# A fourth seven-product unit in gate and up, and low parts formed by adding transfers, in a float32 encoder block on Trainium2

## The chip, the cores and the metric

The kernel is one program on 1 core of one Trainium2 chip. The metric is the device time of one execution in microseconds. TensorE multiplies, VectorE, ScalarE and GpSimd work on data in SBUF (VectorE and ScalarE on PSUM too), SyncE issues the transfers of the weights; GpSimd issues most of the small ones. The engines run side by side, each through its own list of instructions in order, and wait for one another by semaphores.

## The reference, cut to what matters

One layer of an encoder on 256 tokens of width 2048, in float32: four mixers, cross attention, and a gated feed-forward network of width 5632.

```python
def swiglu(h, w_gate_up, w_down):
    gate, up = jnp.split(h @ w_gate_up, 2, axis=-1)
    return (jax.nn.silu(gate) * up) @ w_down

def reference(...):
    mem_n = rms_norm(mem, mem_norm_g)
    ...
    x = x + mix @ w_out[l]
    x = x + cross_attention(rms_norm(x, norm_g[l, 1]), mem_n, w_xq[l], w_xkv[l], w_xo[l])
    x = x + swiglu(rms_norm(x, norm_g[l, 2]), w_gate_up[l], w_down[l])
    return rms_norm(x, final_norm_g)
```

The change lies in `h @ w_gate_up`: 256 x 2048 by 2048 x 11264.

## The kernel before, in words

**Products in three parts.** A float32 operand is split into a high part, rounded to the matmul's format (`wh` for a weight), and a low part, the difference (`wl`). A product is three matmuls: high by high, high by low, low by high (`part`). ScalarE casts the high part (`nc.scalar.copy`), VectorE subtracts for the low part; both are in `Stream.split`.

**The stream of weights.** All weights come through one stream (`Stream`), in the order in which TensorE uses them, as slabs of 128 x 2048 (1 MB). A slab lands in a tile `raw` (three buffers, and in gate and up a fourth for every fourth slab) by a transfer on SyncE's queue, and is split in parts. A plain slab has two parts of 1024 columns; each part takes a buffer for `wh` and one for `wl`. In gate and up there are five such pairs: three in pool `wp`, two in `wp2`. `look` makes parts ahead as long as a pair is free. A pair is free again when TensorE has used the part.

**Gate and up.** Eleven groups `j`, each 512 columns of gate and the same 512 of up, for two blocks of 128 tokens; a group runs over eight slabs `i`, each two blocks `k` of 128 rows of the weights by 1024 columns. Four banks of PSUM (`cs`) collect the sums of a group. A plain slab is 2 x 2 x 2 products of 128 x 128 by 128 x 512, 24 matmuls.

**Units of seven.** Some slabs are multiplied as a 2 x 2 block product with seven products for eight (`unit`, `take_forms`): 21 matmuls. Sums of blocks of the weights are formed by VectorE in place in `raw` (`make`: one step on 1024 columns, two on 512), and the slab is split in four parts, of 512, 1024, 1024 and 1024 columns. Sums of blocks of the activations are formed once, in group 0 (`left`, inside `gate_up`). Four more banks collect what the units of a group share; `combine` adds them up after the last unit. `sevens(j)` says which slabs are units: slab 5 in group 0, slabs 1, 3 and 5 in groups 1 to 10. Units are used in the product with `w_down` as well, which the change leaves alone.

**The end of a group.** `finish` adds `cs` and the units' sums on VectorE, applies SiLU on ScalarE, multiplies, turns the result with VectorE's transpose into a tile `u`, and stores it by GpSimd's queue to `hidden` in DRAM in eight transfers (`store_turned`). It belongs to the next group's slabs 0 and 1, and must be done before that group's first unit begins, which needs the banks.

**GpSimd's queue.** It carries the stores of `keys`, of `values`, of `hidden` and of `xrows` (the residual, turned, in gate and up), and the reads of those back into SBUF.

**What sets the order.** The kernel is written as one list of steps. Side work is written as generators that are polled between matmuls (`Background`). The framework then orders the instructions of each engine by its own estimate of times; `keep_place` adds a dependency on the instruction just ahead on the same engine, so that a step stays where it was written. The steps of the units are kept so; the parts of plain slabs in gate and up are not. The keys are the first product of the kernel: three `gemm_rows` over `w_xkv`, the first with two columns of 512, whose four banks are turned by four transposes in `store_turned`, kept in place.

Of the kernel before, what the change touches and what calls it, by code (L numbers as in the profile page):

```python
# [14 lines left out]
F32R = mybir.dt.float32r  # L15
# [3 lines left out]
ALU = mybir.AluOpType  # L19
# [3 lines left out]
P = 128  # L23
# [25 lines left out]
GU = 16 * (40 + 16 + 16 + 32 + 16)  # L49

def sevens(j):

    return (1, 3, 5) if j else (5,)


FORMED = 6
# [20 lines left out]
DOWN = GU // 16 + 16 * DFF // 1024  # L77
# [6 lines left out]
def seven(slab):  # L84

    j, i = divmod(slab - GU // 16, 8)
    return slab in UNITS if slab >= DOWN else j >= 0 and i in sevens(j)
# [19 lines left out]
PI_LO = float(np.nextafter(np.float32(math.pi), np.float32(0)))  # L107


class Stream:  # L110


# [32 lines left out]
                return pool  # L145
        return None

    def split(self, pool, at, r, edges):

        nc = self.nc  # L150
        wh, wl = (pool.tile([P, 1088], F32R, name=t, tag=t) for t in ("wh", "wl"))
        wh, wl = wh[:, at:at + 1024], wl[:, at:at + 1024]
        for a, b in zip(edges, edges[1:]):
            nc.scalar.copy(wh[:, a:b], r[:, a:b])  # L154
            nc.vector.tensor_tensor(out=wl[:, a:b], in0=r[:, a:b], in1=wh[:, a:b].bitcast(F32), op=ALU.subtract)  # L155
        self.bg.dve(edges[-1], len(edges) - 1)
        self.items.append((pool, wh, wl))

    def make(self):

        nc, (slab, part) = self.nc, self.todo
        n = 16 * slab + 8 * part
        if n >= NBLK - HELD:
            parts = [(self.places.pop(0)) for _ in range(2)]
            r = self.raw(slab)[:, part * 1024:part * 1024 + 1024]
            for a, (wh, wl) in zip((0, 512), parts):
                nc.scalar.copy(wh, r[:, a:a + 512])
                nc.vector.tensor_tensor(out=wl, in0=r[:, a:a + 512], in1=wh.bitcast(F32), op=ALU.subtract)
            self.bg.dve(1024, 2)
            self.items.append((None, parts))  # L170
            self.todo = (slab + part, 1 - part)
            return True
        pool = self.free(slab)
        if pool is None:
            return False
        raw = self.raw(slab)
        at = 48 if any(a <= n < b for a, b in ROWS) else 8
        r = raw[:, part % 2 * 1024:part % 2 * 1024 + 1024]
        if not seven(slab):
            mark = len(nc.cur_bb.bb.instructions)  # L180
            self.split(pool, at, r, [0, 256, 512, 1024] if n == 0 else [0, 512, 1024] if n == 8 else [0, 1024])
            if DOWN <= slab < DOWN + 2 * AHEAD:
                self.keep(mark)
            self.todo = (slab + part, 1 - part)
            return True
        mark = len(nc.cur_bb.bb.instructions)
        op = lambda out, a, b, what=ALU.subtract: nc.vector.tensor_tensor(out=out, in0=a, in1=b, op=what)  # L187
        self.split(pool, at, r, [0, 512] if part == 0 else [0, 1024])
        b11, b12, b22, b21 = (raw[:, a:a + 512] for a in range(0, 2048, 512))
        if part == 0:  # L190
            blk = raw.rearrange("p (b c) -> p b c", b=4)
            op(r.rearrange("p (b c) -> p b c", b=2), blk[:, 0:3:2, :], blk[:, 1:2, :].to_broadcast([P, 2, 512]))
            self.bg.dve(1024)
        elif part == 1:
            op(b22, b22, b11, ALU.add)
            op(b21, b21, b22)
            self.bg.dve(1024, 2)
        self.keep(mark)
        self.todo = (slab + part // 3, (part + 1) % 4)
        return True  # L200
# [87 lines left out]
class Block:  # L288
# [286 lines left out]
    def mixers(self):  # L575
        tc, nc, act = self.tc, self.nc, self.act
# [76 lines left out]
        with tc.tile_pool(name="mid", bufs=1) as mid:  # L653
            self.dgp = mid
            gl = Gla(self, mid)
            with tc.tile_pool(name="hyp", bufs=1) as hyp, tc.tile_pool(name="k2", bufs=8) as k2:
                hy = Hyena(self, hyp, k2)

                mem0 = hy.piece()[:, 0:R + 16]
                nc.sync.dma_start(mem0, self.t["mem0"])  # L660
                self.bg.add(prepare(mid))

                for cols in ([0, 512], [1024], [1536]):
                    first = dict(parts=[[k] for k in range(KT)], before=start_m) if len(cols) > 1 else {}
                    for c, ps in zip(cols, self.gemm_rows("w_xkv", cols, h, **first)):
                        for r in range(2):
                            self.store_turned(self.kd[c:c + 512, r * P:(r + 1) * P], hy.piece(), ps[r][:, :], True)
                    if first:
                        for k in range(0, KT, 4):
                            self.load_x(k, 4)  # L670
                for hd in range(4):
                    for r, p in enumerate(self.gemm_rows("w_xkv", [D + hd * 512], h, start_x if hd == 3 else rows.append)[0]):
                        for c in range(2):
                            v, o = self.tmp(), (2 * hd + r) * 512 + c * R
                            nc.scalar.activation(v, p[:, c * R:(c + 1) * R], AF.Copy, scale=self.rcm[:, r:r + 1])
                            nc.gpsimd.dma_start(self.vd[:, o:o + R], v)
                self.bg.drain()

                def ev_u(i, p):
                    hy.feed(i, self.merge(p))  # L680
                    if i == 4:
                        self.bg.add(hy.convs())

                self.gemm("w_in", [UH + i * P for i in range(12)], h, ev_u)
                for r, p in enumerate(self.gemm_rows("w_in", [512], h, lambda k: k or low_rank())[0]):
                    nc.scalar.copy(gl.v[r], p)
                self.gemm("w_in", [256, 384, 0, 128], h, lambda i, p: gl.feed(i, self.merge(p)))
                self.gemm("w_in", scols[0:NSC], h, ev_s, narrow=True)
                self.bg.drain()

            with tc.tile_pool(name="glp", bufs=1) as glp:
                gl.open(glp)
                fn = Fnet(self, glp, act[20:24])
                g_gla = self.bg.add(gl.mix(act[4:8]))
                fn.feed(self.gemm_rows("w_in", [UF], h)[0])
                g_fn = self.bg.add(fn.mix(act[0:4], gl))
                self.gemm("w_in", scols[NSC:], h, lambda i, p: ev_s(i + NSC, p))
                g_sc = self.bg.add(self.group_norm(self.res[1], 2, act[20:24]))

                def ev_gate(i, p):  # L700
                    nc.scalar.activation(gl.gate[i], p[:, 0:R], AF.Silu)

                self.gemm("w_in", [1024 + i * P for i in range(4)], h, ev_gate, narrow=True)
                gl.done = True
                self.out_proj(lambda n: [self.bg.drain(g) for g in ((g_gla,), (g_fn, g_sc), ())[n]])
# [245 lines left out]
    def gate_up(self, sw, gp, f):  # L951

        nc, st = self.nc, self.st
# [6 lines left out]

        def left():

            for i in (5, 1, 3):
                t = [self.tmp() for _ in range(2)]
                for x, k in zip(t, (2 * i, 2 * i + 1)):
                    nc.scalar.activation(x, self.resk(k), AF.Copy, scale=self.gvec(V_NG + 32, k))
                (a11, a21), (a12, a22) = ((x[:, 0:P], x[:, P:R]) for x in t)
                s = gp.tile([P, 512], F32, name="u", tag="u", bufs=2)
                s1, s2, s3, s4 = (s[:, a:a + P] for a in range(0, 512, P))
                self.stt(s1, a21, -1.0, a22, ALU.mult, ALU.subtract)  # L970
                self.stt(s2, s1, -1.0, a11, ALU.mult, ALU.subtract)
                self.tt(s3, a11, a21, ALU.subtract)
                self.tt(s4, a12, s2, ALU.subtract)
                yield
                h, l = sums[i] = [sw.tile([P, 512], F32R, name=f"s{x}{i}") for x in "hl"]
                self.split2(h, l, s)
                yield
# [44 lines left out]

        ready = [self.late, self.bg.add(norm())]
        forms = self.bg.add(left())
        turned = self.bg.add(self.turn())
        early = end = None
        for j in range(DFF // 512):
# [5 lines left out]
            for i in range(8):  # L1033
# [7 lines left out]
                if i in sevens(j):  # L1041
                    if i == sevens(j)[0]:
                        if j == 0:
                            self.bg.drain(forms)
                        ps = [banks[1 - j % 2]() for _ in range(4)]
# [6 lines left out]
                for k in (2 * i, 2 * i + 1):  # L1052
                    for c in range(2):
                        wh, wl = st.take("w_gate_up", k, cols[c], 4)
# [804 lines left out]
```

## Time and profile before

| | |
|---|---|
| median of 3 runs | 1458.29 us (1456.57 to 1458.53) |
| the profiled execution | 1457.18 us |
| its span | 1455.3 us |
| TensorE busy | 1440.2 us, 99% of the span |
| VectorE busy | 1192.2 us, 82% |
| ScalarE busy | 844.1 us, 58% |
| GpSimd busy | 172.2 us, 12% |
| granted TensorE clock, mean | 0.997 |

In the rows of the profile PE is TensorE's matmul, PEld its loading of weights, DVE VectorE, ACT ScalarE, POOL GpSimd, SP SyncE. A row of the timeline has its start in us from the start of the span, its duration, the engine, the line of the kernel, the operation, the tile written and those read, and in brackets the idle time ahead of it with what ended it. Durations of matmuls overlap: their pace is read from their starts. A row of a stretch has its length and the busy time of each engine in it, the granted clock, and the share and rate of the transfers. A row of transfers has the tile, the queue, the number, the size of one and the median us from issue to landing. Matmuls into `pg` and `pm` are those into two sets of four banks, between which the groups of gate and up alternate.

### The profile page before, as it was taken

How to read it: one execution, taken by the hardware profiler on the slowest of the kernel's cores; microseconds unless marked ns; L12 is line 12 of the kernel's file. 1: busy time of each engine (PE TensorE's matmuls, PEld its weight loads, DVE VectorE, ACT ScalarE, POOL GpSimd, SP SyncE). 2: the span in 40 equal slices, each digit the busy share in tenths (PEclk: the TensorE clock that was granted, in tenths of full speed). 3: DMA queues.
4: the chain of work that ended last, by engine and by line, in shares of the span. 5: the costliest groups of instructions: out<-in, count | busy, mean ns of one | idle time of the engine just before them, and what ended most of it. 6: DMA issues, size and time to landing. Idle time of an engine off the chain costs nothing.

```text
span 1455.3 us, 19732 instructions
## 1 busy us (share of the span) xinstructions
PE 1440.2 (99%) x7219; PEld 1217.8 (84%) x7219; DVE 1192.2 (82%) x1748; ACT 844.1 (58%) x1252; POOL 172.2 (12%) x294
## 2 busy tenths in 40 slices
PE   9999999999999999999999999999999999999997
PEld 7788888888899888888888888888888888788886
DVE  6577768777868867877778999999999997988875
ACT  6466665456646656665555565555555654655554
POOL 0220100000000001110003334112111112100000
PEclk9999999999999999999999999999999999999999
DMA  9885654444535555555556767656667656545554
GB/s 351 283 314 192 229 193 169 174 158 167 206 122 203 204 200 203 185 174 177 199 191 221 252 234 245 241 191 244 234 228 248 207 198 235 216 183 200 224 203 145
DMA packets 57394, 307.16 MB, mean 211 GB/s; under 512 B 9774, under 2 KB 11471, under 8 KB 25681
## 3 DMA queue, kind: packets, MB, share of 16 engines
q1 hardware_dynamic: 45920, 281.11, 54.2%
q0 software_dynamic: 10944, 24.14, 5.5%
q8 instruction: 56, 0.92, 0.2%
q10 hardware_dynamic: 432, 0.66, 0.1%
q14 instruction: 42, 0.34, 0.1%
HBM read 291.71 MB, written 14.16 MB: 210 GB/s over the span
## 4 chain that ended last, share of the span: by engine, by line
PE 96%; DVE 2%; ACT 1%; issue 0%; DMA 0%; SPq 0%; ACTq 0%; DVEq 0%
PE pg L439 19%; PE pg L490 13%; PE pg L491 13%; PE pg L492 13%; PE pg L440 10%; PE pm L490 7%; PE pm L492 7%; PE pm L491 7%; PE pm L1360 1%; DVE wl L155 1%; PE pg L436 1%; PE pg L437 1%; PE pm L890 1%; PE pm L863 1%; ACT wh L154 0%
## 5 line engine op out<-in xcount | busy, mean ns | idle before, releaser
L154 ACT CAST wh<-raw 128x1024 fp32r<-128x1024 f32 (+1 forms) x589 | 589.2, 1013 | 473.1 <-PE pg L492 147.3
L155 DVE TENSOR_TENSOR wl<-raw,wh 128x1024 fp32r<-128x1024 f32 (+1 forms) x589 | 681.8, 1176 | 183.7 <-ACT wh L154 178.0
L439 PE MATMUL pg<-act,wh 128*128 128x512 f32 x1104 | 387.5, 393 | 0.0
L440 PE MATMUL pg<-act,wl 128*128 128x256 f32 x1216 | 340.7, 280 | 0.0
L490 PE MATMUL pg<-wh,act 128*128 128x512 f32 (+1 forms) x689 | 269.6, 392 | 2.3 <-DVE k L520 2.0
L491 PE MATMUL pg<-wl,act 128*128 128x512 f32 (+1 forms) x689 | 268.8, 390 | 1.2 <-DVE wl L155 1.1
L492 PE MATMUL pg<-wh,act 128*128 128x512 f32 (+1 forms) x689 | 268.8, 390 | 0.0
L439 PEld LDWEIGHTS pg<-act,wh 128*128 128x128 f32 x1104 | 207.4, 188 | 45.0
L440 PEld LDWEIGHTS pg<-act,wl 128*128 128x128 f32 x1216 | 228.5, 188 | 0.8 <-DVE wl L155 0.5
L490 PEld LDWEIGHTS pg<-wh,act 128*128 128x128 f32 x689 | 129.7, 188 | 31.0 <-ACT dgh L410 2.4
L491 PEld LDWEIGHTS pg<-wl,act 128*128 128x128 f32 x689 | 129.6, 188 | 29.2 <-DVE wl L155 2.5
L492 PEld LDWEIGHTS pg<-wh,act 128*128 128x128 f32 x689 | 129.7, 188 | 27.3
L491 PE MATMUL pm<-wl,act 128*128 128x512 f32 x318 | 123.7, 389 | 0.0
L492 PE MATMUL pm<-wh,act 128*128 128x512 f32 x318 | 123.7, 389 | 0.0
L490 PE MATMUL pm<-wh,act 128*128 128x512 f32 x318 | 123.6, 389 | 0.0
L187 DVE TENSOR_TENSOR raw<-raw 128x1024 f32<-128x1024 f32 x129 | 111.8, 866 | 3.0
L525 POOL DMA_DIRECT2D hidden<-u x88 | 56.8, 653 | 164.6 <-DVE u L520 141.9
L492 PEld LDWEIGHTS pm<-wh,act 128*128 128x128 f32 x318 | 59.7, 188 | 12.5
L491 PEld LDWEIGHTS pm<-wl,act 128*128 128x128 f32 x318 | 59.7, 188 | 12.4
L490 PEld LDWEIGHTS pm<-wh,act 128*128 128x128 f32 x318 | 59.7, 188 | 12.4
L1072 POOL DMA_DIRECT2D xrows<-tmp x64 | 37.0, 585 | 183.5 <-DVE rc L321 126.6
L936 POOL DMA_DIRECT2D tmp<-hidden x44 | 24.5, 560 | 141.2 <-DVE f L317 73.0
(353 smaller groups left out, 1773.1 us busy)
## 6 DMA issues: line engine op xcount, KB each, us to landing
raw<-in_W SPq DMA_DIRECT2D x246, 1024.0 KB, 4.9
raw<-in_W SPq DMA_DIRECT2D x11, 512.0 KB, 7.5
hidden<-u POOLq DMA_DIRECT2D x88, 64.0 KB, 4.4
tmp<-hidden POOLq DMA_DIRECT2D x44, 128.0 KB, 4.2
res<-in_xT SPq DMA_DIRECT2D x8, 512.0 KB, 7.5
k<-in_mem SPq DMA_DIRECT2D x8, 256.0 KB, 6.5
k<-in_x SPq DMA_DIRECT2D x8, 256.0 KB, 7.7
keys<-k POOLq DMA_DIRECT2D x32, 64.0 KB, 5.3
```

The lines of the kernel that those rows point to most:

```text
L154: nc.scalar.copy(wh[:, a:b], r[:, a:b])
L155: nc.vector.tensor_tensor(out=wl[:, a:b], in0=r[:, a:b], in1=wh[:, a:b].bitcast(F32), op=ALU.subtract)
L187: op = lambda out, a, b, what=ALU.subtract: nc.vector.tensor_tensor(out=out, in0=a, in1=b, op=what)
L436: self.nc.tensor.matmul(p[:, 0:R], wh, slot[:, 0:R], start=start, stop=False)
L439: self.nc.tensor.matmul(p[:, :], wh, slot[:, :], start=start, stop=False)
L440: self.nc.tensor.matmul(p[:, 0:R], wl, slot[:, 0:R], start=False, stop=stop)
L490: self.nc.tensor.matmul(p, hi, wh, start=start, stop=False)
L491: self.nc.tensor.matmul(p, hi, wl, start=False, stop=False)
L492: self.nc.tensor.matmul(p, lo, wh, start=False, stop=stop)
L525: nc.gpsimd.dma_start(to[:, :, 32 * a:32 * a + 32], u[32 * a:32 * a + 32, :].rearrange("f (b t) -> f b t", t=32))
L936: self.nc.gpsimd.dma_start(m[k], self.ff[k * P:(k + 1) * P, :])
L1072: nc.gpsimd.dma_start(to[:, :, c:c + 32], u[32 * a:32 * a + 32, :].rearrange("t (b f) -> t b f", f=32))
```

## The change

Three edits.

In groups 1 to 10 of gate and up slab 4 becomes a unit; `left` forms the sums of activations for it.

In the same groups the second half of each plain slab (0, 2, 6 and 7; `added`) gets its low part without VectorE: ScalarE writes the negated and rounded weights into `wl`, and a transfer on GpSimd's queue adds the unrounded weights from `raw` to it, in SBUF. ScalarE's cast into `wh` comes after the negation. The first halves keep VectorE's subtraction.

In the keys, the four transposes of the first `gemm_rows` are no longer kept in their place.

```diff
 def sevens(j):
-    return (1, 3, 5) if j else (5,)
+    return (1, 3, 4, 5) if j else (5,)

+def added(slab):
+    j, i = divmod(slab - GU // 16, 8)
+    return j >= 1 and slab < DOWN and i not in sevens(j)

-    def split(self, pool, at, r, edges):
+    def split(self, pool, at, r, edges, added=False):
         nc = self.nc
         wh, wl = (pool.tile([P, 1088], F32R, name=t, tag=t) for t in ("wh", "wl"))
         wh, wl = wh[:, at:at + 1024], wl[:, at:at + 1024]
+        if added:
+            nc.scalar.mul(wl, r, -1.0)
+            nc.gpsimd.dma_start(wl, r.bitcast(F32R), accum_op=ALU.add)
+            nc.scalar.copy(wh, r)
+            self.items.append((pool, wh, wl))
+            return
         for a, b in zip(edges, edges[1:]):
...
-            self.split(pool, at, r, [0, 256, 512, 1024] if n == 0 else [0, 512, 1024] if n == 8 else [0, 1024])
+            self.split(pool, at, r, [0, 256, 512, 1024] if n == 0 else [0, 512, 1024] if n == 8 else [0, 1024], part == 1 and added(slab))
...
-                            self.store_turned(self.kd[c:c + 512, r * P:(r + 1) * P], hy.piece(), ps[r][:, :], True)
+                            self.store_turned(self.kd[c:c + 512, r * P:(r + 1) * P], hy.piece(), ps[r][:, :], not first)
...
-            for i in (5, 1, 3):
+            for i in (5, 1, 3, 4):
```

## The prediction

> **What bounds the kernel now.** I read the engines' shares first, then the stage that is changed in stretches of 50 us, then single instructions at one border between two of its groups.
>
> ```profile
> span 1455.3 us, 19732 instructions
> PE 1440.2 (99%) x7219; PEld 1217.8 (84%) x7219; DVE 1192.2 (82%) x1748; ACT 844.1 (58%) x1252; POOL 172.2 (12%) x294
> PE 96%; DVE 2%; ACT 1%; issue 0%; DMA 0%; SPq 0%; ACTq 0%; DVEq 0%
> ```
>
> ```profile
> core 0: us, PE busy (x) PEld busy (x) DVE busy (x) ACT busy (x) POOL busy (x), PEclk, DMA share, GB/s
> 900.00:950.00 50.00, 50.00 (x222) 41.38 (x222) 47.11 (x54) 28.01 (x31) 12.59 (x21) 1.00 0.67 236
> 950.00:1000.00 50.00, 50.00 (x222) 41.39 (x221) 47.34 (x55) 28.38 (x33) 7.45 (x12) 1.00 0.66 233
> ```
>
> TensorE never rests in gate and up, so a matmul taken out is time, and so is every wait put in. VectorE is at 47.3 of 50 us: it has no room for a fourth unit unless something is taken off it. The order in time at one border (TensorE, VectorE, ScalarE, GpSimd):
>
> ```profile
> 921.35 0.39 PE L492 MATMUL pm<-wh,act 128*128 128x512 f32 x1
> 921.58 0.39 PE L490 MATMUL pg<-wh,act 128*128 128x512 f32 x1
> 926.79 0.39 PE L492 MATMUL pg<-wh,act 128*128 128x512 f32 x1
> 927.01 0.39 PE L490 MATMUL pm<-wh,act 128*128 128x512 f32 x1
> ...
> 912.52 1.22 DVE L155 TENSOR_TENSOR wl<-raw,wh 128x1024 fp32r<-128x1024 f32 x1
> 913.65 0.68 DVE L317 TENSOR_TENSOR h<-pg,m 128x512 f32<-128x512 f32 x1
> 914.25 0.68 DVE L317 TENSOR_TENSOR g<-pg,m 128x512 f32<-128x512 f32 x1
> ...
> 919.74 0.69 DVE L317 TENSOR_TENSOR g<-pm,g 128x512 f32<-128x512 f32 x1 [0.79 <-PE pm L492]
> ...
> 928.09 1.29 DVE L520 STREAM_TRANSPOSE u<-h 128x512 f32<-128x512 f32 x2
> 929.31 2.92 DVE L155 TENSOR_TENSOR wl<-raw,wh 128x1024 fp32r<-128x1024 f32 x3
> ...
> 937.46 2.66 ACT L154 CAST wh<-raw 128x1024 fp32r<-128x1024 f32 x3 [0.22 <-PE pg L492]
> ```
>
> ```profile
> 929.09 5.28 POOL L525 DMA_DIRECT2D hidden<-u  x8 [18.91 <-DVE u L520]
> 938.69 0.58 POOL L936 DMA_DIRECT2D tmp<-hidden  x1 [4.32 <-DMA hidden<-u]
> ```
>
> The reader is to see four things. A matmul costs 0.2265 us (24 of them from 921.58 to 927.01). A back-to-back VectorE step costs 1.13 us on 1024 columns and 0.60 on 512. The new group starts at T = 921.58; its slab 0 has 24 matmuls, unit 1 has 21, slab 2 starts at 927.01 + 21 x 0.2265 = 931.77, its second half at 934.5. And GpSimd's queue is taken by the eight stores of the finished group from T+7.5 to T+12.8, because they hang on VectorE's chain of finishing steps, which waits for TensorE at 919.74. The split runs ahead of TensorE only as far as its five buffers (three in wp, two in wp2) go: the cast at 937.46 waits for TensorE to leave slab 2 at 931.77 + 5.44 = 937.21.
>
> **The unit.** In groups 1 to 10 slab 4 turns from 24 matmuls to 21: 10 x 3 x 0.2265 = 6.8 us less on TensorE, all of it on the path. VectorE per group: slab 4 before 2 x 1.13; as a unit 0.60 + 3 x 1.13 of low parts, 1.13 + 2 x 0.60 of sums, 6.3 us. Four plain slabs lose a low part each, 4 x 1.13. Net 6.3 - 2.3 - 4.5 = -0.5 us on some 39: the mean is no worse. The sums for i = 4 in group 0 (four steps on 128 columns and a split of 512, about 2 us of VectorE) lie in a stage with plain slabs, where a slab asks 2.3 us of VectorE for 5.44 of TensorE: nothing; 2 us if that cover is gone.
>
> **The run of three units.** Units at 3, 4, 5 stand next to each other; each asks 6.3 us of VectorE and gives TensorE 21 x 0.2265 = 4.76. Let U be the start of unit 3, with its four parts ready and all buffers full. VectorE starts on unit 4 at U+0.9 (the buffer that slab 2 leaves, cast, subtract) and by the steps above reaches the low part of unit 5's third part at U+11.4, done U+12.5; TensorE wants it at U+9.52+2.04+0.23 = U+11.8. Wait 0.8 us. ScalarE makes it worse in half of the groups: in the changed kernel's order of instructions groups 2, 4, 6, 7 and 9 have casts or the negation for slabs 6 and 7, 1.05 us each, ahead of unit 5's last one or two parts; working the same steps through gives waits of 2.5 to 3.9 us there.
>
> ```profile
> L154 ACT CAST wh<-raw 128x1024 fp32r<-128x1024 f32 x541 | 560.8, 1049 | 447.2 <-PE pg L492 138.9 <-PE pg L439 83.6 <-DVE raw L187 74.4
> hidden<-u POOLq DMA_DIRECT2D x88, 64.0 KB, 4.4
> tmp<-hidden POOLq DMA_DIRECT2D x44, 128.0 KB, 4.2
> values<-tmp POOLq DMA_DIRECT2D x16, 128.0 KB, 2.8
> res<-xrows POOLq DMA_DIRECT2D x8, 256.0 KB, 4.8
> out_x<-res SPq DMA_DIRECT2D x6, 256.0 KB, 3.0
> raw<-in_W SPq DMA_DIRECT2D x246, 1024.0 KB, 4.9
> ```
>
> **The adding transfers.** Forty of them (slabs 0, 2, 6, 7 of ten groups), 512 KB each, SBUF to SBUF. No transfer of this kind is in the trace. From below: 2.8 to 3.0 us from issue to landing (the quickest of these rows). From above: 256 KB on the same queue take 4.8, 0.6 more than 128 KB; two more such steps give 6.0 for 512 KB, and if the reading of the destination counts as another 512 KB, 8.4; I keep 9 as the upper end. I take L = 6, nearest to the row of the same queue.
>
> Each is issued by GpSimd's queue behind what stands there. In nine of the ten groups slab 2's transfer is queued behind the eight stores (in group 6 ahead of them). So it is issued at T+12.8 and lands at T+12.8+L; TensorE wants the low part at its second matmul, T+12.9+0.23. Wait L - 0.3 = 5.7 us, nine times: 51 us. Nothing else stands between: the chain that sets the stores' start (finish, unit 1, the transposes) is step for step that of before.
>
> Slab 6's transfer: the buffer is free when TensorE leaves unit 5's first part, U+10.2+0.25; ScalarE's negation stands behind its casts and ends, in the groups where these come first (1, 3, 5, 8, 10), at about U+14.7; landing U+14.7+L; wanted at U+15.1+2.72+0.23 = U+18.05. Wait 2.6, after the 0.8 above (3.5 to 4.3 by group). In the other five the waits in unit 5 cover it. Mean over the ten groups 3.6: 36 us. Slabs 7 and 0 have 5.4 us more each and land in time at L = 6; the cover is gone at about 9.
>
> ScalarE's forty negations and the unit's 1.75 casts more per group fit: 28.4 of 50 us, or 23.5 of a group, becomes 29.4. The raw slab is held until the transfer lands (slab 2: T+18.8 rather than about T+10); the load into it (4.9 us) is wanted for slab 6 at about T+30. The transfers' traffic lies beside loads at a DMA share of 0.67. Stores behind three transfers wait for no one on the path; reads of hidden are for the next stage.
>
> **First keys' order.** Before, TensorE waits here:
>
> ```profile
> 50.78 1.23 DVE L155 TENSOR_TENSOR wl<-raw,wh 128x1024 fp32r<-128x1024 f32 x1
> 51.92 2.50 DVE L520 STREAM_TRANSPOSE k<-pg 128x512 f32<-128x512 f32 x4
> ...
> 50.40 0.39 PE L492 MATMUL pg<-wh,act 128*128 128x512 f32 x1
> 52.78 0.54 PE L490 MATMUL pg<-wh,act 128*128 128x512 f32 x1 [1.99 <-DVE k L520]
> 53.11 0.63 PE L491 MATMUL pg<-wl,act 128*128 128x512 f32 x1
> 53.54 0.63 PE L492 MATMUL pg<-wh,act 128*128 128x512 f32 x1
> 53.97 0.63 PE L490 MATMUL pg<-wh,act 128*128 128x512 f32 x1
> ```
>
> Freed, the four transposes come ahead of the small norm steps and of the first low part. They run as the banks close (the last at 50.8) and end about 51.6; the low part behind them ends at 52.8, where TensorE now stands for it. The wait changes its name: 0 to -0.3 us, I take 0; -2 and the matmuls at half pace if the low part slips in ahead.
>
> **What a wait costs besides.** After these 2 us matmuls follow at 0.43 us for 3.5 us: 8 x 0.2 = 1.6 us. Nine waits at slab 2 bring 14 us; those in units 5 and slab 6, cut in two, half of it, 8 us. The Trainium skill, TensorE: Matmul & The Clock Gate, Part 1, puts the halved clock after an idle window of about 3.4 us. The row had it after 2.0, so I go by the row; by the page the 8 us would fall away and the 14 stay.
>
> **Sum**, on the profiled execution of 1457.2 us (span 1455.3, 1.1 under the median of 1458.29): -6.8 + 51 + 36 + 14 + 8 = +102; 1559, and 1560 against the median.
>
> **The rivals.**
> *Quick transfers*, L = 3: slab 2 waits 2.7, nine times 24, clock 14; slab 6's transfer is in time but for a few tenths, and unit 5 and its casts leave 22 and clock 4; -6.8: 1457.2 + 57 = 1514. The store rows of 2.8 and 3.0 speak for it, 4.2 to 4.8 on the same queue, in the same stage, against. The Trainium skill, DMA: Bandwidth & Descriptors, Anatomy of one DMA, gives 2.0 us plus bytes at 436 GB/s for this queue, an estimate of 3.2 us for 512 KB and so some 1516 here. The same formula gives 2.6 for 256 KB where the trace has 4.8.
> *Slow transfers*: L = 9 gives 9 x 8.7 = 78 at slab 2, some 56 in units and slab 6, clock 22, less 6.8: 1607; at L = 12 the same steps come near 1665.
> *Only the units wait*: if the scheduled order on GpSimd did no harm (stores done sooner, transfers in time), 22 us of waits in unit 5 and 4 of clock less 6.8: 1477.
> *Faster*: 1457.2 - 6.8 = 1450, 1451.5 by the median. It takes one mechanism: TensorE reaches slab 2's second half after the low part has landed, so the landing must come within 0.3 us of the eighth store. Break-even at slab 2 alone is where nine waits cost the 6.8 gained: L = 0.3 + 6.8/9 = 1.1. No median of these rows is below 2.8, which speaks against it. For it: VectorE's mean load does fall, and the transfers are off the path wherever they are issued in time.
>
> **Chances.** L between 4.5 and 7.5, 1530 to 1588: 0.55. Quick 0.17, slow 0.16 (half of it above 1620). Only units 0.06. Faster 0.05, no change 0.01. The likeliest is 1560; 1490 to 1620 leaves out the last three and half of the cases with L at 9 or above, 2 in 10. A difference under 0.2%, 2.9 us, could not be told from none (the three runs spread over 2.0 us): faster 0.05, same 0.01, slower 0.94.
>
> **What would show it.** Right: TensorE waiting at the second matmul of slab 2's second half in nine groups for the adding transfer, 5 to 6 us each, a granted clock of about 0.95 through the stage for 1.00; in group 6 no such wait; 10 x 3 matmuls fewer; groups of some 50 us for 41.4; waits for low parts in unit 5; first keys as long as before. Wrong: eight stores that start before T+7 or transfers that land in under 2 us; or waits for slabs 7 and 0 as well, when transfers take more than 9.

## The result and the profile after

The changed kernel takes 1561.76 us (median of 4 runs, 1561.47 to 1562.01) against 1457.43 us (1455.13 to 1458.53) for the kernel before on the same chip: a ratio of 1.072, with a 95% interval of 1.0705 to 1.0732. It is 104 us slower; 1560 was forecast. The sum of the forecast was right to 2 us; its terms were not.

The first lines of the profile of the changed kernel, the shares of its chain of waits, and groups 1 to 10 of gate and up as one stretch:

```profile
span 1559.7 us, 19878 instructions
PE 1473.4 (94%) x7189; PEld 1221.8 (78%) x7189; DVE 1194.6 (77%) x1763; ACT 894.6 (57%) x1315; POOL 209.1 (13%) x334
PE 69%; DMA 9%; DVE 9%; issue 7%; POOL 3%; ACT 2%; POOLq 0%; SPq 0%; DVEq 0%; ACTq 0%
793.31:1314.80 521.49, 449.35 (x1801) 348.55 (x1800) 396.69 (x463) 283.32 (x323) 127.70 (x189) 0.94 0.75 222
```

The same stretch in the kernel before:

```profile
797.13:1211.90 414.77, 414.77 (x1831) 343.47 (x1830) 394.95 (x455) 235.82 (x266) 92.27 (x151) 1.00 0.65 228
```

All of the loss is in these ten groups: 521.5 us for 414.8, +106.7. What lies ahead of gate and up became 3.8 us shorter (group 0 starts at 749.92 us, before at 753.73), group 0 is as long as it was, and the rest of the kernel is 1.5 us longer. There are 30 matmuls fewer, as counted. TensorE is busy for 449 of 521 us, the chain, which was TensorE's at 96%, now goes through transfers and VectorE at 9% each, and the granted clock is 0.94 for 1.00. The view of TensorE's waits over the whole kernel (line of the waiting matmul, what it waits for, us in total, times, longest):

```profile
PE pm L503 <- DMA wl<-raw: 27.9, 8, 7.5
PE pg L503 <- DMA wl<-raw: 14.9, 8, 3.6
PE pg L503 <- DVE wl L167: 10.7, 14, 2.2
PE pg L502 <- ACT wh L166: 7.8, 9, 2.1
PE pm L503 <- DVE wl L167: 7.3, 9, 2.2
PE pm L502 <- ACT wh L166: 6.9, 6, 2.1
```

The first two rows are waits for the adding transfers, 42.8 us, all of them in groups 1 to 10. The other four are waits for parts made by VectorE and ScalarE, 32.7 us, of which 29.0 lie in groups 1 to 10; there the kernel before has no wait at all. Put down to the slab and part that the waiting matmul belongs to (by the order of the instructions), the waits for transfers are 3.5 us at slab 0, **2.2 at slab 2**, 26.0 at slab 6 and 11.1 at slab 7; the 29.0 lie in units 3 to 5, 18.1 of them at unit 4's third part.

Why slab 2, which was to cost 51 us, costs almost nothing is seen in the timeline of group 1, which starts at T = 793.31:

```profile
800.82 5.20 POOL L537 DMA_DIRECT2D hidden<-u  x8 [13.43 <-DVE u L532]
806.00 1.00 POOL L161 DMA_DIRECT2D wl<-raw  x1
...
806.23 1.07 PE L502 MATMUL pm<-wh,act 128*128 128x512 f32 x4
...
810.88 0.40 PE L503 MATMUL pm<-wl,act 128*128 128x512 f32 x1
```

The eight stores start at T+7.5 and the transfer is issued at T+12.7, as forecast. TensorE reaches the second half at T+12.9, as forecast too. But then it does only the four matmuls that need the high part alone, goes on with units 3 and 4, and takes up the low part at 810.88, 4.9 us after the issue, when the transfer has just landed (4.7 us). The framework's order had put the other eight matmuls of that half behind matmuls of two units; nothing in the kernel keeps TensorE's matmuls of gate and up in the order in which they are written. The two buffers of slab 2's second half stay occupied meanwhile, so the parts of unit 4 are made later, and the 18 us lie there (with the order kept, below, they are gone).

### The profile page after: what moved, and what is told of

The parts are those of the page before. It is cut to its first block, busy times and chain, and to the rows that moved or that the text cites. A ratio compares the mean times of both kernels' runs of the same rounds, so it can differ in the third digit from the quotient of the medians.

```text
span 1559.7 us, 19878 instructions
## 1 busy us (share of the span) xinstructions
PE 1473.4 (94%) x7189; PEld 1221.8 (78%) x7189; DVE 1194.6 (77%) x1763; ACT 894.6 (57%) x1315; POOL 209.1 (13%) x334
## 3 DMA queue, kind: packets, MB, share of 16 engines
q1 hardware_dynamic: 45920, 281.11, 51.3%
q0 software_dynamic: 16704, 45.11, 12.5%
## 4 chain that ended last, share of the span: by engine, by line
PE 69%; DMA 9%; DVE 9%; issue 7%; POOL 3%; ACT 2%; POOLq 0%; SPq 0%; DVEq 0%; ACTq 0%
PE pg L451 17%; PE pg L503 9%; PE pg L452 9%; PE pg L504 9%; PE pg L502 9%; DMA wl<-raw 6%; DVE wl L167 4%; PE pm L503 3%; PE pm L504 3%; PE pm L502 2%; DVE raw L199 2%; ACT wh L166 2%; DMA raw<-in_W 2%; POOL hidden L537 1%; PE pm L1372 1%
## 5 line engine op out<-in xcount | busy, mean ns | idle before, releaser
L167 DVE TENSOR_TENSOR wl<-raw,wh 128x1024 fp32r<-128x1024 f32 (+2 forms) x569 | 655.8, 1165 | 266.2 <-ACT wh L166 260.4
L166 ACT CAST wh<-raw 128x1024 fp32r<-128x1024 f32 (+2 forms) x569 | 563.5, 1003 | 501.0 <-PE pg L504 158.9
L503 PE MATMUL pg<-wl,act 128*128 128x512 f32 (+1 forms) x664 | 262.6, 396 | 17.1 <-DMA wl<-raw 14.9
L504 PE MATMUL pg<-wh,act 128*128 128x512 f32 (+1 forms) x664 | 261.5, 394 | 0.0
L502 PE MATMUL pg<-wh,act 128*128 128x512 f32 (+1 forms) x664 | 256.0, 392 | 0.9 <-ACT wh L166 0.8
L503 PEld LDWEIGHTS pg<-wl,act 128*128 128x128 f32 x664 | 126.4, 190 | 49.1 <-DMA wl<-raw 18.3
L502 PEld LDWEIGHTS pg<-wh,act 128*128 128x128 f32 x664 | 125.0, 188 | 29.5 <-ACT wh L166 2.9
L504 PEld LDWEIGHTS pg<-wh,act 128*128 128x128 f32 x664 | 126.4, 190 | 26.8 <-issue 0.4
L199 DVE TENSOR_TENSOR raw<-raw 128x1024 f32<-128x1024 f32 x159 | 137.7, 866 | 3.8
L504 PE MATMUL pm<-wh,act 128*128 128x512 f32 x293 | 119.7, 409 | 0.0
L502 PE MATMUL pm<-wh,act 128*128 128x512 f32 x293 | 112.7, 400 | 0.2
L504 PEld LDWEIGHTS pm<-wh,act 128*128 128x128 f32 x293 | 58.9, 201 | 12.5
L502 PEld LDWEIGHTS pm<-wh,act 128*128 128x128 f32 x293 | 56.5, 193 | 14.2 <-ACT wh L166 2.1
L161 POOL DMA_DIRECT2D wl<-raw x40 | 36.3, 908 | 138.4 <-ACT wl L160 74.4
```

Source lines behind the costliest of these rows:

```text
L161: nc.gpsimd.dma_start(wl, r.bitcast(F32R), accum_op=ALU.add)
L502: self.nc.tensor.matmul(p, hi, wh, start=start, stop=False)
L503: self.nc.tensor.matmul(p, hi, wl, start=False, stop=False)
L504: self.nc.tensor.matmul(p, lo, wh, start=False, stop=stop)
```

## The experiments

The kernel before took 1457.3 to 1457.9 us beside each of these. "The changed kernel" below is the one with all three edits.

**The keys' order alone.** The kernel before with the third edit.

```diff
-  self.store_turned(..., ps[r][:, :], True)
+  self.store_turned(..., ps[r][:, :], not first)
```

> The kernel before with the first keys' order freed and nothing else. Theory: the traces put gate and up's start at 753.7 us before and 749.9 after, and the halved clock at 51 us is gone, so this edit is worth 3.8 us: 1453.6. Rival, the prediction's own step: the wait only changes its name, 0 to 0.3 us: 1457.

1453.55 us, ratio 0.9973 (0.9963 to 0.9983): 4 us faster than the kernel before, and the only kernel here that beats it. The rows that answer to those of before (VectorE's transposes and low part, ScalarE's cast, TensorE), from the changed kernel:

```profile
49.50 2.08 DVE L532 STREAM_TRANSPOSE k<-pg 128x512 f32<-128x512 f32 x3
50.86 1.05 ACT L166 CAST wh<-raw 128x1024 fp32r<-128x1024 f32 x1 [1.60 <-PE pg L504]
51.50 2.32 DVE L167 TENSOR_TENSOR wl<-raw,wh 128x1024 fp32r<-128x1024 f32 x2
...
52.24 0.39 PE L503 MATMUL pg<-wl,act 128*128 128x512 f32 x1
52.47 0.39 PE L504 MATMUL pg<-wh,act 128*128 128x512 f32 x1
52.70 0.39 PE L502 MATMUL pg<-wh,act 128*128 128x512 f32 x1
```

The transposes do end at 51.6, as forecast, but TensorE does not stand for the low part behind them: it goes on at full pace. The wait of 1.99 us and eight matmuls at half pace are gone; nothing takes their place.

**The unit alone.** Four units, low parts by VectorE everywhere, the keys' order kept (the edits are against the changed kernel; the keys' line is as before again).

```diff
-  self.split(pool, at, r, [...], part == 1 and added(slab))
+  self.split(pool, at, r, [...], False)
```

> The changed kernel without the adding transfers (VectorE forms all low parts) and with the keys' order kept: the fourth unit alone. Theory (the units themselves cost as well, by VectorE's load and by three in a row): VectorE needs 39.5 + 4.1 = 43.6 us a group where TensorE needs 40.7, so groups of 43 to 45 us for 41.5: 1473 to 1490, with no waits for transfers. Rival (all the loss is the transfers'): 1457.4 - 6.8 = 1451.

1494.72 us, ratio 1.0256 (1.0242 to 1.027), 37 us slower, a little above the theory's range. The unit that saves 6.8 us of TensorE costs 44 us of waits and small delays, because VectorE cannot feed it. Of TensorE's 27.1 us of waits in groups 1 to 10, 18.9 are for ScalarE's casts and 8.2 for VectorE's low parts, but the casts themselves stand 100.8 us there for the sums that VectorE forms in `raw`. Groups 1 to 10 as one stretch:

```profile
796.62:1247.83 451.21, 423.77 (x1802) 333.13 (x1800) 435.54 (x503) 248.35 (x284) 93.35 (x153) 1.00 0.61 210
```

VectorE is at 435.5 of 451.2 us. No wait of TensorE in this kernel is for a transfer.

**Both units and negations, without the transfers.** The changed kernel with line 161 taken out.

```diff
-  nc.gpsimd.dma_start(wl, r.bitcast(F32R), accum_op=ALU.add)
```

> The changed kernel with the adding transfers left out, so that the low part of these halves is only the negated rounded weight: no transfer, no landing, all else stays, though the order on the engines may be set anew. The part of the computation left out is the addition of the unrounded weight. Theory: the waits for transfers (43 us and the clock with most of them) go, those in the units (about 30 us) stay: 1457.4 - 6.8 - 3.8 + 30 + 8 = 1485. Rival (units wait only because the late transfers hold their buffers): 1447 to 1452.

1468.92 us, ratio 1.0082 (1.0067 to 1.0098), between the two expectations. So of the 104 us some 93 (1561.8 less 1468.9) are what the forty transfers cost with all that hangs on them (their place in the queue, their traffic, their landing), and units on relieved engines still cost 15 us against the keys' kernel (1453.6), 22 against that kernel less the 6.8 us of matmuls. The waits in groups 1 to 10 are 12.0 us, 10.6 of them in unit 5, and the clock stays at 1.00:

```profile
793.23:1222.58 429.35, 417.03 (x1801) 335.41 (x1800) 396.23 (x465) 284.10 (x324) 91.66 (x150) 1.00 0.64 220
```

**No three units next to each other.** As the last, with slab 2 a unit in place of slab 3.

```diff
-  return (1, 3, 4, 5) if j else (5,)
+  return (1, 2, 4, 5) if j else (5,)
...
-  for i in (5, 1, 3, 4):
+  for i in (5, 1, 2, 4):
```

> Units at slabs 1, 2, 4 and 5, in two pairs, and the adding transfers left out as in the run without the addition (the part of the computation left out is the addition of the unrounded weight). Theory (the 21 us that are left there come from three units in a row on five buffers): pairs need less of a lead, 1450 to 1458. Rival (four units cost the casts and VectorE as much wherever they stand): 1469, within 4.

1469.11 us, ratio 1.0082 (1.0067 to 1.0097), the same as with the run of three: the rival was right. The forecast had laid the units' waits to three units in a row. It is not the row: four units, in two pairs, wait about as long (11.3 us in groups 1 to 10).

**The transfers alone.** Three units as before, adding transfers in the five plain slabs of each group (fifty in all), the keys' order kept (the keys' line is as before again).

```diff
-  return (1, 3, 4, 5) if j else (5,)
+  return (1, 3, 5) if j else (5,)
...
-  for i in (5, 1, 3, 4):
+  for i in (5, 1, 3):
```

> Three units as before, and adding transfers for the second halves of the five plain slabs (0, 2, 4, 6, 7) of groups 1 to 10; keys' order kept. Theory (transfers that land late, about 6.5 us after issue, are over half of the loss): waits for transfers in slabs 2, 6 and 7 of 40 us or more and the clock with them, 1500 to 1530. Rival (with less to do on VectorE and no run of three units, the transfers land in time): 1457, within 5.

1529.82 us, ratio 1.0494 (1.0479 to 1.0509), at the theory's upper end: 72 us slower with no fourth unit at all. TensorE waits 44.5 us for transfers: 5.8 at slab 0, 5.5 at slab 2, 22.1 at slab 4 and 11.0 at slab 6. The granted clock is 0.96 between 800 and 1200 us.

**Transfers in slabs 0 and 2 only.** The changed kernel, with VectorE's low parts in slabs 6 and 7.

```diff
-  return j >= 1 and slab < DOWN and i not in sevens(j)
+  return j >= 1 and slab < DOWN and i in (0, 2)
```

> Adding transfers for slabs 0 and 2 alone; VectorE forms the low parts of slabs 6 and 7 again, 2.3 us a group more, 40.8 where TensorE needs 40.7. Theory (the waits stand at slabs 6 and 7, 37 us and most of the clock's 24): 1490 to 1515. Rival (what costs is slab 2's late landing, which holds buffers that unit 4 waits for): 1540 or more.

1516.07 us, ratio 1.0405 (1.0389 to 1.042), 1 us above the theory's range: the twenty transfers in slabs 6 and 7 cost 46 us, those in slabs 0 and 2 some 25 (an estimate, against the unit alone less the keys' 4 us, 1491). Inside unit 4 the waits at its third part are still there, 17 us, as the rival had it, though its total of 1540 was not reached.

**GpSimd's queue freed.** The stores of `hidden` and `xrows` and the reads of `xrows` go to SyncE's queue, so that nothing but the reads of `hidden` stands ahead of an adding transfer.

```diff
-  nc.gpsimd.dma_start(to[:, :, 32 * a:32 * a + 32], ...
+  (queue or nc.gpsimd).dma_start(to[:, :, 32 * a:32 * a + 32], ...      # nc.sync for hidden
...
-  nc.gpsimd.dma_start(to[:, :, c:c + 32], ...
+  nc.sync.dma_start(to[:, :, c:c + 32], ...
...
-  nc.gpsimd.dma_start(self.half(c, r), ...
+  nc.sync.dma_start(self.half(c, r), ...
```

> The changed kernel with the stores of hidden, the stores of xrows and the reads of xrows issued on SyncE's queue instead of GpSimd's: nothing stands ahead of the adding transfers but the reads of hidden. Theory (part of the lateness is GpSimd's queue: slab 2 behind eight stores, the two longest waits, 7.5 and 6.7 us at slab 6, behind the residual's transfers): 1510 to 1545. Rival (the transfers are late because ScalarE's negation is late and the landing takes 6.5 us): 1552 to 1565.

1544.82 us, ratio 1.0598 (1.0581 to 1.0616): 17 us less than the changed kernel, at the upper end of what the theory gave. But the gain is not where the theory looked for it. TensorE waits 52.0 us for transfers, more than the 42.8 of the changed kernel, now 12.7 at slab 2, 28.3 at slab 6 and 11.0 at slab 7, and the transfers take 7.8 us from issue to landing in the median, for 6.5. What fell are the waits in the units, from 29.0 to 10.2 us. The stores now stand among the loads on SyncE's queue, so this kernel does not show the place in the queue by itself.

**The order of plain slabs kept.** Two lines around the parts of plain slabs in gate and up.

```diff
+  mark = self.mark()
   ...
+  self.keep_place(mark)
```

> The changed kernel with TensorE's matmuls of the plain slabs in gate and up kept in the order in which they are written (a dependency on the matmul ahead). In the changed kernel the scheduled order puts the low matmuls of slab 2's second half behind work of unit 3. Theory (this moved order is why the prediction's waits of 5.7 us at slab 2 are not there): with the order kept they appear, 6.5 - 0.3 = 6 us in nine groups with the clock, the waits in unit 4 (18 us) shrink: 1595 to 1615. Rival (the wait only moves from unit 4 to slab 2, since the same buffers are held): 1555 to 1570.

1564.55 us, ratio 1.0733 (1.0715 to 1.0751). The number lies in the rival's range, but it tells nothing: with only the plain slabs' matmuls kept, the first matmuls of unit 3 still passed ahead of slab 2's low ones, as in the changed kernel. The next kernel does what this one was to do.

**The order of all of gate and up kept.** The same two lines around the units' matmuls as well, so that TensorE's order is the written one.

> The changed kernel with the matmuls of gate and up, of plain slabs and of units, all kept in the order in which they are written, so that no unit's matmul passes ahead of slab 2's second half. Theory (the forecast's mechanism was right, and the scheduled order moved its price on): the waits of some 5 to 6 us at the low part of slab 2's second half appear in nine groups, 45 to 55 us in all, and the waits for buffers inside unit 4 (18 us in the changed kernel) shrink below 8. The total is then no shorter than the changed kernel's: 1565 to 1610. Rival (the adding transfer of slab 2 lands in time by itself): the waits at slab 2 stay under 10 us in all, the total at 1555 to 1567.

1589.48 us, ratio 1.0908 (1.0887 to 1.0928), as the theory had it. The border of group 2 (T = 845.59):

```profile
853.11 5.22 POOL L537 DMA_DIRECT2D hidden<-u  x8 [15.62 <-DVE u L532]
858.32 0.98 POOL L161 DMA_DIRECT2D wl<-raw  x1
...
858.51 0.39 PE L502 MATMUL pg<-wh,act 128*128 128x512 f32 x1
863.07 0.80 PE L503 MATMUL pg<-wl,act 128*128 128x512 f32 x1 [4.17 <-DMA wl<-raw]
863.66 0.63 PE L504 MATMUL pg<-wh,act 128*128 128x512 f32 x1
864.09 0.63 PE L502 MATMUL pg<-wh,act 128*128 128x512 f32 x1
```

This is the wait that the forecast described, at the matmul that it named: stores at T+7.5, transfer at T+12.7, low part wanted at T+13.1. It stands in all ten groups, 4.1 to 4.2 us in nine and 6.2 in one, 43.4 us in all (just under the 45 expected), and matmuls at half pace (0.43 us for 0.23) follow it. The waits inside unit 4 are gone. The other places changed too: unit 5 waits 20.3 us (5.9 in the changed kernel), slabs 6 and 7 wait 28.7 (37.1). So the mechanism at slab 2 exists; in the changed kernel the scheduled order turned 43 us there into 18 us in unit 4.

**Transfers in halves.** Each adding transfer as two of 512 columns, 256 KB.

```diff
-  nc.gpsimd.dma_start(wl, r.bitcast(F32R), accum_op=ALU.add)
+  for a in (0, 512):
+      nc.gpsimd.dma_start(wl[:, a:a + 512], r[:, a:a + 512].bitcast(F32R), accum_op=ALU.add)
```

> The changed kernel with each adding transfer split in two of 512 columns, 256 KB each, issued one behind the other on the same queue. If the landing time grows with the size (6.5 us at 512 KB), 256 KB land in some 5 us, the first half of a low part is there earlier and the waits for transfers shrink: 1540 to 1555. If most of the landing time and of the waits is the queue and the fixed part of a transfer, the two cost more than the one: both land 6 us or more after their issue and the total is 1562 to 1585.

1554.47 us, ratio 1.067 (1.0637 to 1.0704): 7 us less, at the upper end of the first case by its time; by the landing it is the second, for the median of the 80 halves is 6.7 us. At slab 2, where in most groups no load runs, the first half lands 3.4 us after its issue and the second, issued 0.6 us behind it, mostly 4.3 to 4.7 after its own; so the first half is there earlier than the whole would be (4.6 to 4.7) and the second is not. Waits for transfers fall from 42.8 to 30.5 us, and those for parts in groups 1 to 10 rise from 29.0 to 34.0.

**Copies for additions.**

```diff
-  nc.gpsimd.dma_start(wl, r.bitcast(F32R), accum_op=ALU.add)
+  nc.gpsimd.dma_start(wl, r.bitcast(F32R))
```

> The changed kernel with transfers that copy and do not add: the same 512 KB on the same queue at the same places, so that the low part is the unrounded weight itself (the subtraction is left out of the computation). Theory (the reading of the destination for the addition lengthens the landing of 6.5 us): the copy lands in 4 to 5 us, the waits shrink by 1.5 to 2 us each, and the total is 1505 to 1540. Rival (size and queue set the landing, the addition costs nothing besides): 6 to 7 us and 1555 to 1567.

1542.66 us, ratio 1.0573 (1.0553 to 1.0594), just past the theory's upper end; the landing fell to 4.6 us in the median as the theory said, and the waits for transfers from 42.8 to 27.2 us. From issue to landing of the 40 transfers, in the changed kernel:

```profile
DMA to landing us min/median/max: 4.5/6.5/12.2
```

and with copies:

```profile
DMA to landing us min/median/max: 2.9/4.6/10.0
```

The spread says more than the median. In the changed kernel the transfer of slab 2 lands 4.6 to 4.7 us after its issue in nine groups (copies: 2.9 to 3.1), those of slab 0 in groups 2 to 10 after 8.7 to 12.2 us, slab 7's after 5.3 to 11.3, slab 6's after 4.5 to 5.6 in seven groups, and 10.5, 10.4 and 7.3 in groups 1, 5 and 10. In these three stand the longest waits of slab 6, 7.5, 6.7 and 3.6 us. Group 1's, with the stretch ahead of it:

```profile
832.00:836.00 4.00, 0.04 (x1) 0.04 (x1) 0.00 (x0) 0.00 (x0) 0.00 (x0) 0.50 1.07 218
```

```profile
835.96 0.79 PE L503 MATMUL pm<-wl,act 128*128 128x512 f32 x1 [7.45 <-DMA wl<-raw]
```

The sixteen DMA engines are full (share 1.07) while every compute engine stands: three adding transfers and a load of 1 MB are under way together. What goes with a slow transfer is clearest in the kernel with transfers in slabs 0 and 2 only, where they are far apart. What the queues moved from issue to landing of two of them (packets, MB, share of sixteen engines; q1 is SyncE's queue of loads, q0 GpSimd's), slab 0's issued at 829.42 us and slab 2's at 850.12:

```profile
q1 hardware_dynamic: 320, 2.23, 60.3%
q0 software_dynamic: 144, 0.52, 24.5%
...
wl<-raw POOLq DMA_DIRECT2D x1, 512.0 KB, 10.8
```

```profile
q0 software_dynamic: 197, 0.66, 73.9%
q1 hardware_dynamic: 3, 0.02, 3.1%
wl<-raw POOLq DMA_DIRECT2D x1, 512.0 KB, 4.7
```

Its twenty transfers fall in two groups: ten with at most 0.13 MB of loads meanwhile land in 4.6 to 5.3 us, ten with 0.74 to 2.23 MB in 6.9 to 10.8. In the changed kernel, where others of their kind share the queue as well, the same count has fifteen transfers with at most 0.2 MB of loads, which land in 4.5 to 5.4 us, and twelve with over 1.1 MB, which land in 9.1 to 12.2; the thirteen between take 4.8 to 10.7. This is a correlation: a slow transfer also leaves more time for loads to move, and no kernel here took the loads away.

Over the whole span the queues of the changed kernel show what one costs:

```profile
q1 hardware_dynamic: 45920, 281.11, 51.3%
q0 software_dynamic: 16704, 45.11, 12.5%
```

Before, and with copies for additions:

```profile
q0 software_dynamic: 10944, 24.14, 5.5%
```

```profile
q0 software_dynamic: 16704, 45.11, 9.3%
```

The forty adding transfers add 115 us of all sixteen engines (12.5% of 1559.7 less 5.5% of 1455.3), 2.9 us each; copied, 63 us, 1.6 each. A load of the same 0.52 MB takes 1.5 (51.3% of 1559.7 us for 281 MB). So an adding transfer holds the engines as long as a load twice its size.

## Why the prediction was right, and where it was not

| term | forecast, us | found in the changed kernel, us |
|---|---|---|
| matmuls saved | -6.8 | -6.8 (30 fewer) |
| slab 2's second half | +51 | 2.2; 43.4 where the order is kept |
| units 3 to 5 | } +36 | 29.0, of it 18.1 at unit 4's third part |
| slab 6 | } | 26.0 |
| slabs 0 and 7 | 0 | 14.7 |
| half pace behind waits | +22 | 24 (114 matmuls) |
| first keys | 0 | -3.8 |

These come to 85 of the 104 us. Most of the rest lies in the restarts: measured from start to start, the pauses at waits are some 9 us longer than the idle time that the profile gives them, and some 8 us are short delays that no row puts down to a releaser. Another 1.5 us lie behind gate and up.

By the forecast's own signs its account of this kernel was wrong: the waits of 5 to 6 us at slab 2 are not there, and waits at slabs 7 and 0, which it named as a sign against itself, are.

*Slab 2* is the step that failed, though its mechanism was there. "TensorE wants the low part at its second matmul, T+12.9+0.23" assumed the written order; the changed kernel's own order of TensorE's instructions has four high matmuls there and then a unit. It could have been read from that order before any run, as the forecast did for ScalarE and GpSimd. With the order kept the wait appears at that matmul, at 4.3 us (858.51 to 863.07 less one pace) where the formula L - 0.3 gives 4.4 for the L of 4.7 found there: formula right, L = 6 too high for this transfer. It appears in group 6 as well, because in that kernel group 6's transfer, too, is issued behind the stores (at 1080.65 us, the stores from 1075.46); in the changed kernel it is ahead of them, as the forecast had it (1063.91 and 1064.63).

*L as one number* is the second failing step. 6 was close to the median, 6.5, but the transfers fall into two kinds: some 4.6 us with the DMA engines to themselves, and mostly 7 to 12 beside loads and one another. For that reason "Slabs 7 and 0 have 5.4 us more each and land in time" failed (14.7 us), and 17.8 of slab 6's 26.0 us stand in the three groups where its transfer took 7.3 to 10.5 us, not an even 3.6 in each. That "the transfers' traffic lies beside loads at a DMA share of 0.67" was named and given no price; a mean of 0.67 hid stretches at 1.0. The rival with quick transfers fell on the same point: copies land in 2.9 us when alone, close to its L = 3, and yet the whole takes 1543, not 1514.

*The units*: 22 us over the sum without their waits, found with the transfers taken out (1468.9 against 1453.6 - 6.8), is what the rival "only the units wait" had priced at 22 + 4. The size was right, the reason given (three in a row) was not: the pairs cost the same. What is left, argued and not shown, is that VectorE and ScalarE feed a unit more slowly than TensorE uses it and that five buffers do not bridge it; which of these decides was not separated. With the transfers taken out ScalarE's casts stand 63.1 us in groups 1 to 10 for VectorE's sums in `raw` and 71.3 for buffers that TensorE has still to leave.

*First keys* was wrong by 4 us: the freed transposes did not push the next low part into TensorE's way. TensorE wanted that part later than the forecast had it.

*The clock* was right in size: 22 for 24 us, 0.94 granted for "about 0.95", though most of the waits that brought it stood elsewhere.

So the total is right by luck, because errors met: slab 2 was 49 us too high, and units 3 to 5, slab 6 and slabs 0 and 7 together 34 us too low, with some 19 us of restarts and the like that had no term, 2 us more of half pace, and 4 us of the keys the other way. That the change would be slower, and through late transfers and the units, was not luck.

## What to carry to other kernels

Where a scheduler orders an engine's instructions, read the changed order itself before placing a wait: the order can move the wait, and buffers held meanwhile can cost time elsewhere. A transfer's landing time is not one number: price it by what else the DMA engines carry in that stretch, alone and beside a load. Taking work off one full engine is worth only as much as the slowest hand-off put in its place: here 4.5 us of VectorE per group was replaced by a chain of ScalarE, GpSimd's queue and the DMA engines, and cost nine.

## What the runs showed of the hardware

An adding transfer of 512 KB within SBUF lands in some 4.6 us where no load runs, a copy of the same size in 2.9 to 3.1. The Trainium skill, DMA: Bandwidth & Descriptors, Anatomy of one DMA, gives an estimate of 3.2 us for this size; the copies agree, the additions do not, by 1.5 us. The Trainium skill, DMA: Bandwidth & Descriptors, Queues, rings and completion order, says that each DMA engine goes round between the queues that it has work for, a packet at a time. The traces agree as far as they show that both queues slow down together: beside three adding transfers (slabs 6 and 7 of group 1, slab 0 of group 2) the load issued at 825.64 us took 8.4 us, for a median of 4.9 in the kernel before, and those transfers 10.5 to 12.2. In what order the packets went is not shown.

The halved clock does not follow from a wait's length alone. In the changed kernel no single wait up to 1.6 us was followed by matmuls at half pace, and every one from 2.7 us on was, with 6 to 13. Between these it went both ways: of two waits of 2.58 us the one that ended at 940.61 us was followed by eight, the one that ended at 1200.74 by none. Two stretches of 3.41 us around each of them:

```profile
937.24:940.65 3.41, 0.83 (x5) 0.37 (x3) 1.82 (x2) 3.08 (x4) 0.93 (x2) 1.00 1.07 216
940.65:944.06 3.41, 3.41 (x8) 2.76 (x9) 0.00 (x0) 0.00 (x0) 0.83 (x1) 0.50 1.06 247
```

```profile
1196.65:1200.06 3.41, 1.51 (x7) 0.93 (x5) 2.54 (x3) 3.41 (x5) 0.89 (x1) 1.00 1.06 255
1200.06:1203.47 3.41, 2.73 (x12) 2.27 (x13) 0.43 (x1) 1.22 (x3) 1.44 (x2) 1.00 1.06 214
```

The borders are not chosen freely. In the records of the granted clock of all thirteen kernels here, every one of the 81 halved stretches before TensorE's last matmul lasts one, two or three times 3.41 us and begins on one grid of 3.41 us in its run. The first wait fell into one such window, the second lay across a border, 1.90 us before it and 0.68 behind. Of the windows at full clock, all 71 in which TensorE stood idle for more than 1.90 us were followed by a halved one, 10 of the 30 with 1.61 to 1.90 us, and none of the 5480 with less. The Trainium skill, TensorE: Matmul & The Clock Gate, Part 1, has a window of about 3.4 us that runs freely, and the records agree; it puts the halved clock after an idle window, and here a window that was idle for a little over half of its length was enough.
